# The up-projections of two squared-ReLU layers as seven block products in place of eight

## The chip, the cores and the metric

The kernel runs on one NeuronCore of one Trainium2 chip. The core has five engines that take their own instructions in order and meet only through semaphores: TensorE (PE in the profile; PEld is its weight load), VectorE (DVE), ScalarE (ACT), GpSimd (POOL) and SyncE (SP), which here only issues DMAs. Matrix products read SBUF and write PSUM; DVE and ACT read PSUM and SBUF. The metric is device time in microseconds, the median of the runs.

## The reference

The program is a small encoder trunk over 512 tokens of width 1024: an attention layer and a recurrent (RG-LRU) layer, and after each a dense squared-ReLU MLP with 4096 hidden features. Only the MLP changes:

```
def rmsnorm(x, g):
    y = xf * lax.rsqrt(jnp.mean(xf * xf, axis=-1, keepdims=True) + RMS_EPS)
    return (y * g).astype(x.dtype)

def sq_relu_mlp(h, w1, w2):
    z = jax.nn.relu(jnp.einsum('bsd,df->bsf', h, w1))     # 1024 -> 4096
    return jnp.einsum('bsf,fd->bsd', z * z, w2)           # 4096 -> 1024

for layer in range(2):
    h = h + mixer(layer, rmsnorm(h, norm_mix[layer]))
    h = h + sq_relu_mlp(rmsnorm(h, norm_mlp[layer]), w1[layer], w2[layer])
return rmsnorm(h, norm_final)
```

All inputs are float32.

## The kernel before

**Layout.** The residual stream lies transposed in SBUF: eight tiles `hT[k]` of 128 features by 512 tokens. Every float32 matrix product is done as three products of a shorter float format (`mm3`, L148 to L151): an operand X is split into a high part (a cast, `XH`) and the remainder (`XL`), and a tile of the result is WH·XH + WH·XL + WL·XH, accumulated in PSUM. A matmul instruction multiplies a 128x128 piece of weights (loaded by its own LDWEIGHTS) with 128x512 values, and the result has 512 columns, one per token. So each pass over k of one 128-feature output costs 3 matmuls.

**Norms.** `Norm.feed` is called for each finished `hT[m]`: `split` makes `hnH[m]`, `hnL[m]` (ACT L168, DVE L169) without the factor 1/rms, and `square` adds up the squares. The factor is a vector over tokens; `sums` and `rstd` compute it on PE, ACT and DVE while the next product already runs, and it is applied when a result leaves PSUM.

**Weights.** All weight reads of the program stand in one list, `plan`. `fetch` takes the next unit of 128x1024 values (512 KB): a DMA on SP's queue into one of 3 raw buffers `wr` (L97), the cast to `wh` on ACT (L99), the remainder `wl` on DVE (L100); `wh` and `wl` have 5 buffers each. `want(n)` hands out the next n units and keeps 4 more ahead. The pools of `wr`, `wh` and `wl` are open during the whole program, so the units of a layer's MLP can be fetched while the layer before still runs.

**The MLP** (`mlp`, L485). Four groups of 1024 hidden features. `up(g, u)` computes 256 features of the group: two PSUM tiles, each 8 values of k times 3 matmuls of 512 columns; `relu2` takes each through DVE (L495, max and factor), ACT (L497, square), DVE (L500, cast `zH`) and DVE (L501, remainder `zL`). `down(g, u)` multiplies the group's eight z tiles with w2 and adds the result to two tiles of `hT` (L527). After the first group, `up` of the next group and `down` of this one alternate. In the last layer the last group's `down` runs in two halves of 256 tokens each (matmuls of 256 columns, L556), so that the final norm of the first half can run beside the second.

**Order.** The code is recorded by a tile framework which then places the instructions of each engine by its own estimate of when they can run; at run time each engine takes them strictly in the order placed. Tiles come from pools; a pool that is closed gives its SBUF space to the next one opened, and the first write into that space waits for the last use of the old tiles there. Between the attention layer and MLP 0 stands a short block of 22 tiny vector operations (L457 to L471, pool `sp`), the softplus that the recurrent layer needs later.

PSUM has eight banks, four with the tag `mm` (function `mmp`) and four with the tag `at` (`atp`); attention uses both, the MLP only `mm` and two short-lived `at` tiles for the norm.

Of the kernel before, what the change touches and what calls it, by code (L numbers as in the profile page):

```python
# [40 lines left out]
def trunk(ctx: ExitStack, tc: tile.TileContext, xT, cols, win, wqkv, wo, rwin, rga, rgx, rwo, w1, w2, out):  # L41
# [37 lines left out]

    plan = []  # L80
    state = {"next": 0, "ready": []}
    AHEAD = 4

    def fetch():
        i = state["next"]
        state["next"] += 1
        nk, srcs = plan[i]
        n = nk * sum(src.shape[1] for src in srcs)
        pool = state["extra"] if i >= len(plan) - 3 else wsp
        raw = wraw.tile([P, 1024], F32, name=f"wr{i}", tag="wr")  # L90
        H = pool.tile([P, 1024], F32R, name=f"wh{i}", tag="wh")
        L = pool.tile([P, 1024], F32R, name=f"wl{i}", tag="wl")
        rv = raw[:, :n].rearrange("p (k c) -> p k c", k=nk)
        c0 = 0
        for src in srcs:
            w = src.shape[1]
            nc.sync.dma_start(rv[:, :, c0 : c0 + w], src.rearrange("(k p) c -> p k c", p=P))  # L97
            c0 += w
        S.copy(H[:, :n], raw[:, :n])  # L99
        V.tensor_sub(L[:, :n], raw[:, :n], f(H[:, :n]))  # L100
        state["ready"].append((nk, H[:, :n].rearrange("p (k c) -> p k c", k=nk), L[:, :n].rearrange("p (k c) -> p k c", k=nk)))

    def want(n):
        while len(state["ready"]) < n + AHEAD and state["next"] < len(plan):
            fetch()
# [4 lines left out]
    def add(src, r0, c0, nk):  # L110
        for h in range(0, nk, 4):
            plan.append((4, [src[r0 + h * P : r0 + (h + 4) * P, c0 : c0 + U]]))

    def add_qk(p):
        for part in range(2):
            plan.append((KT, [wqkv[:, part * D + p * P : part * D + (p + 1) * P]]))
# [4 lines left out]
    def add_wo(r):  # L121
        for u in range(2):
            plan.append((2, [wo[r * P : (r + 2) * P, u * T : (u + 1) * T]]))

    for k0, nk in FIRST:
        plan.append((nk, [wqkv[k0 * P : (k0 + nk) * P, part * D : part * D + U] for part in range(2)]))
# [4 lines left out]

    def add_mlp(layer):
        a = [(w1[layer], 0, g * D + u * U, KT) for g in range(4) for u in range(4)]
        b = [(w2[layer], g * D, u * U, KT) for g in range(4) for u in range(4)]
        seq = a[:4]
        for i in range(12):
            seq += [a[4 + i], b[i]]
        for s_ in seq + b[12:]:
            add(*s_)
# [6 lines left out]
    add_mlp(1)  # L146

# [12 lines left out]


    class Norm:
        def __init__(self, name, gain, c0=0, n=T):
            self.name, self.gain, self.acc, self.last, self.c, self.n = name, gain, None, None, slice(c0, c0 + n), n

        def split(self, k):
            g = cst[:, self.gain + k : self.gain + k + 1]
            S.activation(hnH[k], hT[k], AF.Copy, scale=g)  # L168
            V.scalar_tensor_tensor(hnL[k], hT[k], g, f(hnH[k]), ALU.mult, ALU.subtract)  # L169
# [21 lines left out]
        def sums(self):  # L191
            nt = self.n // P
            ss = atp(f"{self.name}ss")
# [10 lines left out]
        def rstd(self):  # L204
            nt = self.n // P
            row = atp(f"{self.name}row")
# [10 lines left out]
    nm1 = Norm("nm1", C_MLP0)  # L217
# [266 lines left out]

    def mlp(ly, norm, nxt, halves):  # L485
        with ExitStack() as mctx:
            zp = mctx.enter_context(tc.tile_pool(name=f"z{ly}", bufs=2))
            if halves:
                state["extra"] = mctx.enter_context(tc.tile_pool(name="wx", bufs=3))
                fin = mctx.enter_context(tc.tile_pool(name="fin", bufs=4))  # L490
            z, r, held = {}, [], []

            def relu2(g, fi, acc):
                t1 = zp.tile([P, T], F32, name=f"t1{ly}{g}{fi}", tag="t1")
                V.scalar_tensor_tensor(t1, acc, 0.0, r[0], ALU.max, ALU.mult)  # L495
                t2 = zp.tile([P, T], F32, name=f"t2{ly}{g}{fi}", tag="t2")
                S.activation(t2, t1, AF.Square)  # L497
                zH = zp.tile([P, T], F32R, name=f"zH{ly}{g}{fi}", tag=f"zH{fi}")
                zL = zp.tile([P, T], F32R, name=f"zL{ly}{g}{fi}", tag=f"zL{fi}")
                V.tensor_copy(zH, t2)  # L500
                V.tensor_sub(zL, t2, f(zH))  # L501
                z[g, fi] = (zH, zL)

            def up(g, u):
                WH, WL = want(2)
                xs = [(hnH[k], hnL[k]) for k in range(KT)]
                accs = [mmp(f"u{ly}{g}{2 * u + i}") for i in range(2)]
                if g == 0 and u == 0:
                    project(accs, PAIR, WH, WL, xs)
                    norm.sums()  # L510
                    held.extend(accs)
                    return
                for i in range(2):
                    project(accs[i : i + 1], PAIR[i : i + 1], WH, WL, xs)
                    if held:
                        r.append(norm.rstd())
                        for fi in range(2):
                            relu2(0, fi, held.pop(0))
                    relu2(g, 2 * u + i, accs[i])

            def down(g, u):
                WH, WL = want(2)
                for i in range(2):
                    m = 2 * u + i
                    acc = mmp(f"d{ly}{g}{m}")
# [218 lines left out]
```

## Time and profile before

| | us |
|---|---|
| median of 3 runs (1113.29 to 1114.4) | 1113.7 |
| the profiled execution | 1114.19 |
| its span, first to last instruction | 1112.1 |
| PE busy | 1095.4 (99%) |
| DVE busy | 665.5 (60%) |
| ACT busy | 443.0 (40%) |
| first and last start of an up-projection matmul, both layers (tile u) | 249.9 to 1043.5 |
| first and last start of a down-projection matmul (tile d) | 306.3 to 1101.6 |
| recurrent layer's products (tiles xb to ro) | 600.0 to 747.6 |

The mean granted TensorE clock of the execution was 0.997 of full speed. A group in the profile is one line, engine, operation and tile name, with count, busy time and mean duration of one; matmuls overlap in the pipeline, so the mean duration of one matmul (389 ns) is longer than the distance from one start to the next, and it is this distance that counts. "Idle before" is what the engine waited, and for whom.

### The profile page before, as it was taken

The page shows a single profiled execution, that of the slowest core. Times are in us where ns is not written, and L with a number is a line of the kernel's source. Part 1 is how long each engine was busy: PE and PEld are TensorE (multiplying, and loading weights), DVE is VectorE, ACT ScalarE, POOL GpSimd, SP SyncE. Part 2 cuts the span into 40 slices and gives each one's busy share as a digit, 9 for nine tenths or more (in the row PEclk, how much of TensorE's full clock was granted, in tenths as well). Part 3 has the DMA queues.
Part 4 walks back from the last instruction along what each step waited for, and adds up shares of the span by engine and source line. Part 5 has one row for each costly group of instructions (what it writes and reads, how often), then busy time and mean ns, then how long its engine had stood idle before and what let it go on. Part 6 is the DMA issues. An engine that isn't in the chain of part 4 may idle for free.

```text
span 1112.1 us, 13697 instructions
## 1 busy us (share of the span) xinstructions
PE 1095.4 (99%) x5368; PEld 926.3 (83%) x5368; DVE 665.5 (60%) x1108; ACT 443.0 (40%) x698; POOL 9.4 (1%) x28
## 2 busy tenths in 40 slices
PE   9999999999999999999999999899999999999997
PEld 7889988878888888888888888788888888888896
DVE  6898887878544444445455889864544454444434
ACT  6766656555322221222234687542312222222311
POOL 1010000000000000000000000000000000000000
PEclk9999999999999999999999999999999999999998
DMA  8433332222332323223233221433233332323302
GB/s 266 134 101 90 107 102 80 92 66 87 94 114 77 114 86 104 95 95 103 87 114 114 76 76 57 132 94 96 87 103 95 95 99 91 114 77 114 105 10 76
DMA packets 112752, 108.95 MB, mean 98 GB/s; under 512 B 4016, under 2 KB 108592, under 8 KB 112688
## 3 DMA queue, kind: packets, MB, share of 16 engines
q1 hardware_dynamic: 112544, 108.02, 31.8%
q8 instruction: 42, 0.69, 0.3%
q14 instruction: 22, 0.18, 0.1%
q10 hardware_dynamic: 144, 0.07, 0.0%
HBM read 101.78 MB, written 2.10 MB: 93 GB/s over the span
## 4 chain that ended last, share of the span: by engine, by line
PE 90%; DVE 6%; ACT 2%; issue 1%; DMA 1%; SPq 0%; DVEq 0%; ACTq 0%
PE d L151 11%; PE d L149 11%; PE d L150 11%; PE u L149 10%; PE u L151 10%; PE u L150 10%; PE x L344 2%; PE xb L149 1%; PE xb L151 1%; PE xb L150 1%; PE wo L149 1%; PE ro L149 1%; PE ro L150 1%; PE ro L151 1%; PE v L149 1%
## 5 line engine op out<-in xcount | busy, mean ns | idle before, releaser
L99 ACT CAST wh<-wr 128x1024 fp32r<-128x1024 f32 (+1 forms) x185 | 193.4, 1048 | 335.8 <-PE d L150 198.0
L100 DVE TENSOR_TENSOR wl<-wr,wh 128x1024 fp32r<-128x1024 f32 (+1 forms) x185 | 225.2, 1218 | 132.6 <-ACT wh L99 131.8
L150 PE MATMUL d<-zL,wh 128*128 128x512 f32 (+1 forms) x576 | 210.6, 366 | 0.0
L149 PE MATMUL d<-zH,wh 128*128 128x512 f32 (+1 forms) x576 | 210.6, 366 | 0.0
L151 PE MATMUL d<-zH,wl 128*128 128x512 f32 (+1 forms) x576 | 210.5, 365 | 0.0
L149 PE MATMUL u<-hnH,wh 128*128 128x512 f32 x512 | 199.7, 390 | 1.4 <-DVE hT L295 1.4
L151 PE MATMUL u<-hnH,wl 128*128 128x512 f32 x512 | 199.2, 389 | 0.0
L150 PE MATMUL u<-hnL,wh 128*128 128x512 f32 x512 | 199.2, 389 | 0.0
L150 PEld LDWEIGHTS d<-zL,wh 128*128 128x128 f32 x576 | 108.7, 189 | 17.6
L151 PEld LDWEIGHTS d<-zH,wl 128*128 128x128 f32 x576 | 108.7, 189 | 17.4
L149 PEld LDWEIGHTS d<-zH,wh 128*128 128x128 f32 x576 | 108.7, 189 | 17.4
L149 PEld LDWEIGHTS u<-hnH,wh 128*128 128x128 f32 x512 | 96.1, 188 | 21.5 <-ACT wh L99 1.8
L151 PEld LDWEIGHTS u<-hnH,wl 128*128 128x128 f32 x512 | 96.1, 188 | 20.1
L150 PEld LDWEIGHTS u<-hnL,wh 128*128 128x128 f32 x512 | 96.1, 188 | 19.9
L497 ACT ACTIVATE t<-t 128x512 f32<-128x512 f32 x64 | 40.4, 633 | 148.5 <-DVE t L495 148.2
L527 DVE TENSOR_TENSOR hT<-d,hT 128x512 f32<-128x512 f32 x56 | 38.7, 692 | 81.2 <-PE d L151 81.2
L495 DVE SCALAR_TENSOR_TENSOR t<-u,nm2r 128x512 f32<-128x512 f32 x32 | 22.0, 691 | 57.2 <-PE u L151 51.4
L495 DVE SCALAR_TENSOR_TENSOR t<-u,nm1r 128x512 f32<-128x512 f32 x32 | 22.0, 691 | 55.7 <-PE u L151 51.4
L501 DVE TENSOR_TENSOR zL<-t,zH 128x512 fp32r<-128x512 f32 x64 | 44.3, 692 | 2.0
L324 ACT ACTIVATE p<-p,mx 128x128 f32<-128x128 f32 (+1 forms) x64 | 35.2, 552 | 15.1 <-DVE mx L321 15.0
L500 DVE CAST zH<-t 128x512 fp32r<-128x512 f32 x64 | 27.1, 423 | 21.4 <-ACT t L497 21.2
L149 PE MATMUL v<-wh,hnH 128*128 128x256 f32 x128 | 36.7, 287 | 0.0
(292 smaller groups left out, 1568.4 us busy)
## 6 DMA issues: line engine op xcount, KB each, us to landing
wr<-in_w SPq DMA_DIRECT2D x128, 512.0 KB, 3.7
wr<-in_wqkv SPq DMA_DIRECT2D x20, 512.0 KB, 3.9
wr<-in_rwin SPq DMA_DIRECT2D x16, 512.0 KB, 3.5
wr<-in_wo SPq DMA_DIRECT2D x8, 512.0 KB, 3.5
wr<-in_rwo SPq DMA_DIRECT2D x8, 512.0 KB, 3.4
hT<-in_xT SPq DMA_DIRECT2D x8, 256.0 KB, 4.7
bias<-in_win SPq DMA_DIRECT2D x4, 512.0 KB, 4.2
kh<-kh SPq DMA_DIRECT2D x16, 128.0 KB, 2.3
```

The costliest lines, as they stand in the source:

```text
L99: S.copy(H[:, :n], raw[:, :n])
L100: V.tensor_sub(L[:, :n], raw[:, :n], f(H[:, :n]))
L149: PE.matmul(acc, WH, XH, start=start, stop=False)
L150: PE.matmul(acc, WH, XL, start=False, stop=False)
L151: PE.matmul(acc, WL, XH, start=False, stop=stop)
L324: S.activation(pt[:, seg[t] : seg[t] + n], pt[:, seg[t] : seg[t] + n], AF.Exp, bias=mx[:, t : t + 1], accum_out=sm[:, t : t + 1],)
L344: PE.transpose(b[:, c : c + P], pt[:, seg[t] + kt * P : seg[t] + (kt + 1) * P], ident)
L495: V.scalar_tensor_tensor(t1, acc, 0.0, r[0], ALU.max, ALU.mult)
L497: S.activation(t2, t1, AF.Square)
L500: V.tensor_copy(zH, t2)
L501: V.tensor_sub(zL, t2, f(zH))
L527: V.tensor_add(hT[m], acc, hT[m])
```

## The change

**Blocks.** The 4096 hidden features are worked in eight groups of 512 (before: four of 1024). For a group, the weight block (1024 inputs x 512 features) is cut into four quarters of 512 x 256, and the tokens and inputs of the normed stream into four quarters of 512 inputs x 256 tokens. In place of eight products of quarters, seven products are made (one level of Strassen's scheme), of sums of weight quarters with sums of stream quarters; the four quarters of the result are sums of the seven.

**Weight sums.** `plan` now names a kind per unit. For a group, the unit "11" issues four DMAs into four raw tiles `b11`, `b21`, `b22`, `b12` (pool `sr`, one buffer each, open only during the MLP). The kinds "s1", "s2", "s4" add raw tiles in place on DVE (L115, L116: four additions of 128x1024 in all), and each of the seven kinds is then cast and split like any unit (ACT L118, DVE L119). So a group has 7 units of w1 in place of 4; w2 has 4 units per 512 features as before. `wh` and `wl` get 4 further buffers (pool `wx`), 7 units are kept ahead in place of 4, and a `stop` mark keeps `fetch` from taking an MLP's units before that MLP begins: `prefetch(6)` stands at its start, after the pools are opened.

**Stream sums.** `Norm.split` of the tiles k < 4 works in halves of 256 tokens and stores first half and difference of the halves (L208 to L211); `sums_of`, four times at the start of each MLP, makes three further sums and their splits (L541 to L556).

**Products.** `product` (one of seven) makes two result tiles of 128 features x 256 tokens, each 4 values of k times 3 matmuls of 256 columns: 24 matmuls. `up(g)` runs the seven and adds their results up on DVE (7 operations of 512 columns) and ACT (one copy, `w`); `relu2` runs twice per group on 1024 columns, the cast `zH` now on ACT. The seven products use the `at` banks. `down(g, m)` sums over 4 z tiles in place of 8, so it runs twice as often, and so does the addition to `hT`. The order of a group on PE is p1, p5, two downs of the group before, p2, down, p4, down, p6, down, p3, down, p7, two downs.

```diff
     def fetch():
...
+        kind, nk, srcs = plan[i]
+        pool = wsp
+        if state["more"] is not None:
+            pool = state["more"] if state["units"] % 9 >= 5 else wsp
+            state["units"] += 1
...
+            if kind == "11":
+                for name, src in zip(("11", "21", "22", "12"), srcs):
+                    raws[name] = state["raw"].tile([P, 1024], F32, name=f"b{name}_{i}", tag=f"b{name}")
+                    nc.sync.dma_start(raws[name].rearrange("p (k c) -> p k c", k=4), src.rearrange("(k p) c -> p k c", p=P))
+
+            for name, at_, with_ in (("s1", "21", "22"), ("s2", "22", "11"), ("s4", "12", "22")):
+                if kind == name:
+                    if kind == "s1":
+                        V.tensor_add(raws["11"], raws["11"], raws["21"])
+                    V.tensor_add(raws[at_], raws[at_], raws[with_])
+            raw = raws[{"s1": "21", "s2": "22", "s3": "11", "s4": "12"}.get(kind, kind)]
         S.copy(H[:, :n], raw[:, :n])
         V.tensor_sub(L[:, :n], raw[:, :n], f(H[:, :n]))
...
+    def prefetch(n):
+        while len(state["ready"]) < n and state["next"] < len(plan) and state["next"] != state["stop"]:
+            fetch()
+
     def want(n):
-        while len(state["ready"]) < n + AHEAD and state["next"] < len(plan):
-            fetch()
+        prefetch(n + state["ahead"])
...
     def mlp(ly, norm, nxt, halves):
         with ExitStack() as mctx:
...
+            sr, wx, zp, tp, cp = pool("sr", 1), pool("wx", 4), pool("z", 2), pool("t", 1), pool("c", 1)
+            state.update(raw=sr, more=wx, units=0, ahead=7, stop=starts[ly + 1] if ly + 1 < len(starts) else None)
+            prefetch(6)
...
+            def sums_of(k):
...
+                V.scalar_tensor_tensor(raw[:, 2], hT[k + 4][:, HI], g2, a[:, HI], ALU.mult, ALU.subtract)
+                V.tensor_add(raw[:, 1], raw[:, 2], a[:, LO])
+                V.scalar_tensor_tensor(raw[:, 0], hT[k + 4][:, LO], g2, raw[:, 1], ALU.mult, ALU.subtract)
+                S.activation(H[:, 0:2], raw[:, 0:2], AF.Copy, scale=-1.0)
+                V.scalar_tensor_tensor(L[:, 0:2], raw[:, 0:2], -1.0, f(H[:, 0:2]), ALU.mult, ALU.subtract)
+                S.copy(H[:, 2], raw[:, 2])
+                V.tensor_sub(L[:, 2], raw[:, 2], f(H[:, 2]))
...
+            def product(acc, xs):
+                WH, WL = want(1)
+                for j in range(2):
+                    for k, (XH, XL) in enumerate(xs):
+                        mm3(acc[:, j * U : (j + 1) * U], WH(k, PAIR[j]), WL(k, PAIR[j]), XH, XL, k == 0, k == 3)
...
+                one("1", B11)
+                S.copy(w, acc["1"])
+                yield
+                one("5", t1)
+                yield
+                one("2", B21)
+                V.tensor_add(cA[:, :, LO], acc["2"], w)
+                yield
+                one("4", t4)
+                yield
+                one("6", t2)
+                V.tensor_add(w, acc["6"], w)
+                V.tensor_add(cA[:, :, HI], acc["5"], w)
+                yield
+                one("3", B22)
+                V.tensor_add(cA[:, :, HI], acc["3"], cA[:, :, HI])
+                relu2(g, 0, cA, ALU.max, r[0])
+                yield
+                one("7", t3)
+                V.tensor_add(w, acc["7"], w)
+                V.tensor_add(cB[:, :, LO], acc["4"], w)
+                V.tensor_add(cB[:, :, HI], acc["5"], w)
+                relu2(g, 1, cB, ALU.min, r[0])
```

**How the change moves instructions.** First place: SP's queue at the end of the attention layer (kh, kl are the last copies of attention; wr is a raw buffer; the number after a name tells one buffer's contents from another's). Before:

```order
L253 DMA kl70_2235<-kl70_2235 64x512 [waits DVE_49]
L253 DMA kl71_2241<-kl71_2241 64x512 [waits DMAHW2_49,DVE_49]
L97 DMA wr33_2546<-in_w1 128x4x256 [waits DMAHW4_49,DVE_49]
L97 DMA wr34_2605<-in_w1 128x4x256 [waits DMAHW5_49,DVE_49]
L97 DMA wr35_2672<-in_w1 128x4x256 [waits DMAHW6_49,DVE_49]
```

Now:

```order
L295 DMA kl71_2241<-kl71_2241 64x512 [waits DMAHW2_49,DVE_49]
L104 DMA wr42_3007<-in_w2 128x4x256 [waits DMAHW4_49,DVE_49]
L104 DMA wr44_3075<-in_w2 128x4x256 [waits DMAHW5_49,DVE_49]
L104 DMA wr47_3186<-in_w2 128x4x256 [waits DMAHW6_49,DVE_49]
L110 DMA b11_33_2839<-in_w1 128x4x256 [waits DMAHW1_49,DMAHW2_49,DMAHW0_49,DMAHW7_49,DVE_49,Activation_49]
L110 DMA b21_33_2841<-in_w1 128x4x256
L110 DMA b22_33_2843<-in_w1 128x4x256
L110 DMA b12_33_2845<-in_w1 128x4x256
```

Before, the first reads of MLP 0's w1 wait for raw buffers that the units of the attention layer's last projection set free. Now the first read of w1 is `b11_33`, and its wait on DVE counts, in the built program, up to L512, the operation of the softplus block that reads that block's pool last: the tiles of `sr` lie where the pools of attention and the pool `sp` lay.

Second place: VectorE at the start of MLP 0, now (tL are splits of the stream sums, sp4 and sp8 the end of the softplus block, wl33 the remainder for p1, wl34 for p5, wl35 for p2, wl36 for p4, wl37 for p6):

```order
L554 SCALAR_TENSOR_TENSOR tL03_2912<-ht03_2913,tH03_2911 128x512 [waits Activation_49]
L510 TENSOR_TENSOR sp4_103<-sp4_103,sp2_2787 128x8 [waits DVE_49]
L512 SCALAR_TENSOR_TENSOR sp4_103<-sp4_103,sp1_2786 128x8 [waits DVE_49]
L513 TENSOR_SCALAR sp8_104<-sp4_103 128x8 [waits DVE_49]
L119 TENSOR_TENSOR wl33_2838<-b11_33_2839,wh33_2837 128x1024 [waits DMAHW6_49,Activation_49]
L115 TENSOR_TENSOR b11_33_2839<-b11_33_2839,b21_33_2841 128x1024 [waits DMAHW7_49,DVE_49]
L116 TENSOR_TENSOR b21_33_2841<-b21_33_2841,b22_33_2843 128x1024 [waits DMAHW0_49,DVE_49]
L119 TENSOR_TENSOR wl34_2850<-b21_33_2841,wh34_2849 128x1024 [waits Activation_49]
L119 TENSOR_TENSOR wl35_2856<-b12_33_2845,wh35_2855 128x1024 [waits DMAHW1_49,Activation_49]
L119 TENSOR_TENSOR wl36_2860<-b22_33_2843,wh36_2859 128x1024 [waits Activation_49]
L116 TENSOR_TENSOR b22_33_2843<-b22_33_2843,b11_33_2839 128x1024 [waits DVE_49]
```

All four `sums_of` and the whole softplus block stand ahead of the first weight remainder; before, five units of w1 (wl33 to wl37, L100) stood ahead of the softplus block's second operation. On ACT likewise the cast `wh33` stands behind the last cast of the stream sums. In MLP 1 the same `b11` (unit 145) waits for the last matmul of `ro7`, the recurrent layer's output product, and ACT's `wh145` and DVE's `wl145` stand among the first two stream sums.

Third place: VectorE late in a middle group, now (group 4 of MLP 0; p7 is the seventh product, d036 and d037 the last two downs of group 3, zL041 the second remainder of z of group 4, which the first down of group 4 reads):

```order
L618 TENSOR_TENSOR w04_4304<-p704_4605,w04_4304 128x512 [waits PE_49]
L119 TENSOR_TENSOR wl90_4644<-b22_84_4437,wh90_4643 128x1024 [waits Activation_49]
L619 TENSOR_TENSOR cB04_4303<-p404_4457,w04_4304 128x2x256 [waits DVE_49]
L620 TENSOR_TENSOR cB04_4303<-p504_4337,w04_4304 128x2x256
L632 TENSOR_TENSOR hT6_80<-d036_4648,hT6_80 128x512 [waits PE_49]
L578 SCALAR_TENSOR_TENSOR cB04_4303<-cB04_4303,nm1r_3041 128x1024 [waits DVE_49]
L119 TENSOR_TENSOR wl91_4681<-wr91_4682,wh91_4680 128x1024 [waits DMAHW5_49,Activation_49]
L632 TENSOR_TENSOR hT7_81<-d037_4662,hT7_81 128x512 [waits PE_49]
L116 TENSOR_TENSOR b12_84_4439<-b12_84_4439,b22_84_4437 128x1024
L583 TENSOR_TENSOR zL041_4640<-cB04_4303,zH041_4639 128x1024 [waits Activation_49]
```

Between the end of p7 and `zL041` DVE now takes nine operations: four of the group's own sums and `relu2`, two additions to `hT`, two weight remainders and one weight addition. Before, a z tile's remainder followed its product after one operation on PSUM and a cast.

195 lines of the change are left out of this document (114 added, 81 removed).

## The prediction

> **What bounds the kernel now.** I read the page first, then who made TensorE wait, then the middle of the MLP.
>
> ```profile
> span 1112.1 us, 13697 instructions
> PE 1095.4 (99%) x5368; PEld 926.3 (83%) x5368; DVE 665.5 (60%) x1108; ACT 443.0 (40%) x698; POOL 9.4 (1%) x28
> PE 90%; DVE 6%; ACT 2%; issue 1%; DMA 1%; SPq 0%; DVEq 0%; ACTq 0%
> ```
>
> The chain of waits that ended last is 90% TensorE. The waits of TensorE alone, longest first:
>
> ```profile
> PE ro L149 <- ACT gdH L649: 1.6, 1, 1.6
> PE ro L149 <- DVE y L644: 1.5, 1, 1.5
> PE u L149 <- DVE hT L295: 1.4, 1, 1.4
> ```
>
> In both MLPs there is one wait that counts, 1.4 us at the start of the first. Between 300 and 600 us (windows: span, then busy us of PE, PEld, DVE, ACT, POOL, clock, DMA share, GB/s) TensorE is never idle, while VectorE works 139.83 of 300 us:
>
> ```profile
> 300.00:600.00 300.00, 300.00 (x1325) 248.51 (x1324) 139.83 (x171) 80.70 (x94) 0.00 (x0) 1.00 0.31 96
> ```
>
> So matmul columns are the time, as long as the other engines keep up. The change gives TensorE fewer columns and VectorE more work; the questions are what a column costs in shorter matmuls, and where VectorE's cover ends.
>
> **Matmuls removed.** The distance from start to start counts, not the duration. From the timeline, 20 starts of 512 columns and 53 of 256 columns:
>
> ```profile
> 499.62 0.39 PE L150 MATMUL u<-hnL,wh 128*128 128x512 f32 x1
> ...
> 503.92 0.39 PE L151 MATMUL d<-zH,wl 128*128 128x512 f32 x1
> ```
>
> ```profile
> 1069.72 0.28 PE L149 MATMUL d<-zH,wh 128*128 128x256 f32 x1
> ...
> 1075.96 0.28 PE L150 MATMUL d<-zL,wh 128*128 128x256 f32 x1
> ```
>
> 4.30/19 = 226.3 ns and 6.24/52 = 120.0 ns, each matmul with its own weight load. Per 512 features the up-projection had 4 x 8 x 3 = 96 matmuls of 512 columns, 21.7 us; now 7 x 24 = 168 of 256 columns, 20.2 us (one product 2.88). That is 1.56 us per group, 25.0 us for 16 groups, where an eighth of the columns would be 2.7 per group: a matmul of 256 columns takes 6.9 ns more than half of one of 512. `down` keeps its columns (one `down` of 12 matmuls: 2.72 us), but in the last layer only the last 512 features run in halves: 96 matmuls of 512 and 192 of 256 (21.7 + 23.0) for 384 of 256 (46.1), 1.3 us less. **Together -26.3 us.**
>
> [...]
>
> **VectorE and ScalarE in a middle group.** Rows by form, and stretches of VectorE's timeline, where operations behind each other start closer than their duration:
>
> ```profile
> L100 DVE TENSOR_TENSOR wl<-wr,wh 128x1024 fp32r<-128x1024 f32 x183 | 223.8, 1224 | 132.3 <-ACT wh L99 131.5
> L99 ACT CAST wh<-wr 128x1024 fp32r<-128x1024 f32 x183 | 192.2, 1052 | 335.7 <-PE d L150 198.0 <-PE u L150 90.9 <-PE wo L150 11.5
> L500 DVE CAST zH<-t 128x512 fp32r<-128x512 f32 x64 | 27.1, 423 | 21.4 <-ACT t L497 21.2
> ```
>
> ```profile
> 240.92 1.89 DVE L295 TENSOR_TENSOR hT<-wo,hT 128x512 f32<-128x512 f32 x3 [0.84 <-PE wo L151]
> ...
> 253.39 0.74 DVE L169 SCALAR_TENSOR_TENSOR hnL<-hT,cst,hnH 128x512 fp32r<-128x512 f32 x1
> 254.06 0.68 DVE L182 TENSOR_TENSOR nm1acc<-nm1acc,nm1sq 128x512 f32<-128x512 f32 x1
> 254.66 0.68 DVE L295 TENSOR_TENSOR hT<-wo,hT 128x512 f32<-128x512 f32 x1
> ...
> 255.33 1.22 DVE L100 TENSOR_TENSOR wl<-wr,wh 128x1024 fp32r<-128x1024 f32 x1
> 256.47 0.16 DVE L458 TENSOR_TENSOR sp<-cst,sp 128x8 f32<-128x8 f32 x1
> ...
> 259.16 0.17 DVE L460 TENSOR_SCALAR sp<-sp 128x8 f32<-128x8 f32 x1
> ...
> 264.51 0.17 DVE L471 TENSOR_SCALAR sp<-sp 128x8 f32<-128x8 f32 x1
> ...
> 1105.53 3.22 DVE L553 SCALAR_TENSOR_TENSOR nf1o<-hT,cst,nf1row 128x256 f32<-128x256 f32 x8 [1.32 <-PE nf1row L208]
> ```
>
> Steps: 1.14 us for 1024 columns, 0.60 for a sum of 512, 0.66 for a scaled one of 512, 0.40 for a scaled one of 256, some 0.35 for a plain one of 256. A group now has on VectorE 11 remainders, 4 weight sums, 2 `relu2` and 2 zL of 1024 columns (19 x 1.14 = 21.7) and 7 sums of products and 8 additions to hT (15 x 0.60 = 9.0): 30.7 us, against 20.2 + 21.7 = 41.9 us of TensorE. ScalarE has 15 operations of 1.05 and a copy, 16.4 us. So in the middle neither is the bound. The tightest chain is z: behind p7 VectorE's nine operations and zL take 8.7 us (4 x 1.14 and 5 x 0.60 as in the third place shown, and zL 1.14); TensorE has until then two downs, p1, p5 and half a down, 5.4 + 5.8 + 1.4 = 12.6 us. Casts stand some 20 us ahead of their product. I take **0** here; without the cover of 3.9 us each us would cost 14 us over the run.
>
> **Start of MLP 0.** Here the change moves work into a place where nothing covers it. TensorE's last wo matmul and first u matmul now:
>
> ```profile
> 248.08 0.39 PE L151 MATMUL wo<-oH,wl 128*128 128x512 f32 x1
> ...
> 249.90 0.47 PE L149 MATMUL u<-hnH,wh 128*128 128x512 f32 x1 [1.44 <-DVE hT L295]
> ```
>
> In the changed order the first w1 read waits for the end of the softplus block, and that stands on VectorE behind all norm rows and all stream sums. From the first hT addition (240.9): 15 sums of 512 (9.0), 4 differences of 256 (1.4), 8 scaled of 256 (3.2) and 4 scaled of 512 (2.6) end the norm at 257.1. Stream sums: four times 0.40 + 0.35 + 0.40 + 0.66 + 0.35 = 8.6. The 20 softplus rows from 259.16 to 264.51 took 5.5 us less one wl, 4.4; between other work they cost between 0.08 and 0.2 each, I take 2.8. With 0.8 for waits on ACT (one table load), the read is issued at **269.3**. Then:
>
> ```profile
> wr<-in_w SPq DMA_DIRECT2D x128, 512.0 KB, 3.7
> 10.00:15.00 5.00, 5.00 (x22) 3.85 (x21) 5.00 (x8) 5.00 (x9) 0.00 (x0) 1.00 1.04 363
> ```
>
> About 4 us for `b11` (four reads of 2.1 MB at 363 GB/s: 5.8 us), 1.05 for the cast: p1 can begin at 274.5, its third matmul waits for wl33 until 275.8; p5 waits for two weight sums, a cast and a remainder, until 280.6. From there VectorE leads: until zL of group 0 it has 26 operations of 1024 columns for 11 units and sums of two groups and w2 units (18 wl, 8 sums), 8 of 512, and 4 for relu2 and zL: 30 x 1.14 + 8 x 0.60 = 39 us, starting 5.3 after the read, and some 5 of waits on casts and on group 1's reads, whose buffers come free only now: until 49.7 us after the read. TensorE's work in that time is 11 products, 30 matmuls of 512 and the norm's 0.9: 39.4. Lost: 269.3 - 248.3 = 21.0, and 10.3; less the 1.6 lost now: **+29.7 us**. Bounds: softplus rows hidden and no waits, 22; durations in place of steps, 39.
>
> The clock is no further cost:
>
> ```profile
> 1103.00:1106.00 3.00, 1.84 (x10) 1.49 (x10) 0.64 (x3) 0.26 (x1) 0.00 (x0) 0.74 0.00 0
> 1106.00:1112.00 6.00, 0.00 (x0) 0.00 (x0) 2.75 (x8) 0.00 (x0) 0.00 (x0) 0.50 0.52 175
> ```
>
> An idle TensorE falls to 0.50, so p1 may take 5.8 us; it then ends when p5's remainder is ready.
>
> **Start of MLP 1.** `b11` waits only for the last ro matmul. From there VectorE has the last hT, hnL and sum (2.0), the stream sums (8.6), the same 30 operations of 1024 (34.2) and 8 of 512 (4.8): 49.6, some 2 of waits, against TensorE's 39.4: **+12 us** (bounds 8, if TensorE's rows fall better between; 20, by durations). Now nothing is lost there.
>
> **Ends.** Behind group 7 each down takes 2.72 us, and VectorE has 1.86 per tile for hT, hnL and the squares, beside zL and some remainders: nearly full. 0 to 4, taken as **+2**.
>
> **Sum.** -26.3 + 29.7 + 12 + 2 = +17.4 on the profiled execution's 1114.2 (span 1112.1; 0.5 above the median of 1113.7): 1131.6; on the median's scale **1131 us**.
>
> **Rivals.** (a) VectorE binds in the middle too: zL later than 12.6 us behind p7. For it: VectorE at 73% of the time, in strict order, with waits on casts between. Against: 3.9 us of slack. At 2 us in each of 14 groups: 1159. (b) Faster: the starts cost less than the 26.3 gained. The mechanism would be that VectorE takes sums that touch only SBUF at the rate of the CAST row (423 ns for 512 columns): stream sums and weight sums fall by 40%, 7 us at each start, which with the low bounds (22 and 8) leaves 16: 1114.2 - 26.3 + 16 = 1104. The nm1acc row, SBUF only, 0.68 us for 512, speaks against it. It decides once both starts together cost under 26.3 us. (c) The shorter matmuls don't pay: above 226.3 x 96/168 = 129 ns the seven products are a loss. At 188 ns (the mean of a weight load, were it not hidden) +158 us, 1315. Against: 120.0 measured, weights changing each time. [...]
>
> **Numbers.** Forecast 0.80, with its bounds as the range: 1114.2 - 26.3 + 22 + 8 + 0 = 1118, and 1114.2 - 26.3 + 39 + 20 + 4 = 1151, on the median's scale 1117 to 1151. (a) 0.10; (b) 0.07; (c) 0.01; 0.02 that the starts cost just what the matmuls gain and the time stays within 0.2% (2.2 us, about what a measurement of this kernel can tell from no change). The forecast's low edge adds 0.01 to that. Faster 0.07, same 0.03, slower 0.90. The range leaves out (b), (c) and the larger part of (a), under 2 in 10.
>
> **What would show it.** PE's waits: `p1..` of MLP 0 on DMA, ACT or DVE for over 20 us, a gap of some 26 us behind wo; at MLP 1 some 6 us and pieces on wl. In the middle windows PE full and DVE near 75%. Starts of the products' matmuls 120 ns apart. DVE busy for some 900 us in all: 665, and 48 more remainders and 64 weight sums (112 x 1.22 = 137), 112 sums of products and 64 additions to hT of 512 columns (some 120), less a third of the old relu2 and zH. I would be wrong if the first w1 read came long before 265 us, or if TensorE waited for zL or wl in every group.

## The result, and the profile after

The changed kernel takes **1130.96 us** (median of 4 runs, 1128.77 to 1133.38); the kernel before, in the same runs, 1113.61 us (1113.29 to 1114.4). The ratio is **1.0155, 95% interval 1.0133 to 1.0178**: slower. Predicted were 1131 us, range 1117 to 1151. The profiled execution took 1131.64 us, with a mean granted clock of 0.982 (0.997 before).

The page of the changed kernel: the span, the busy time of each engine, the shares of the chain that ended last.

```profile
span 1129.8 us, 16086 instructions
PE 1080.1 (96%) x6424; PEld 962.4 (85%) x6424; DVE 880.6 (78%) x1324; ACT 537.7 (48%) x794; POOL 10.5 (1%) x28
PE 84%; DVE 10%; ACT 2%; DMA 2%; issue 2%; DVEq 0%; ACTq 0%; SPq 0%
```

TensorE is busy for 15.3 us less than before (1095.4), and the span is 17.7 us longer: what the shorter matmuls saved was more than lost again in idle time. TensorE's share of the chain fell from 90% to 84%, VectorE's rose from 6% to 10%. Whom TensorE waited for (us in total, times, longest):

```profile
PE p L180 <- ACT wh L118: 32.5, 4, 24.7
PE p L182 <- DVE wl L119: 3.4, 5, 1.3
```

In the MLPs the kernel before had one wait of 1.4 us, at the start of MLP 0, and no other ahead of the final norm. Now one wait of 24.7 us stands there. The timeline around it, row by row from four engines: VectorE's softplus row for which the read waits (L512), SP's queue with the first w1 read, ScalarE's cast, VectorE's remainder and TensorE's p1:

```profile
267.53 0.17 DVE L512 SCALAR_TENSOR_TENSOR sp<-sp,sp 128x8 f32<-128x8 f32 x1
...
267.76 2.02 SPq L110 DMA_DIRECT2D b<-in_w  x4
...
271.85 1.04 ACT L118 CAST wh<-b 128x1024 fp32r<-128x1024 f32 x1 [5.25 <-DMA b<-in_w]
...
272.93 1.23 DVE L119 TENSOR_TENSOR wl<-b,wh 128x1024 fp32r<-128x1024 f32 x1 [5.02 <-ACT wh L118]
...
272.95 0.58 PE L180 MATMUL p<-hnH,wh 128*128 128x256 f32 x1 [24.70 <-ACT wh L118]
```

The read is issued 0.2 us behind the start of that softplus row, as the order had said, and 4.1 us later the cast starts. Windows of the changed kernel (span, then busy us of PE, PEld, DVE, ACT, POOL; clock, DMA share, GB/s): the gap, the middle of each MLP, and two short stretches that come back below, one in MLP 0 and one at the start of MLP 1:

```profile
249.00:275.00 26.00, 1.59 (x5) 1.30 (x6) 20.67 (x60) 13.56 (x23) 0.00 (x0) 0.57 0.24 78
340.00:590.00 250.00, 250.00 (x1573) 226.98 (x1572) 187.13 (x201) 96.08 (x98) 0.00 (x0) 1.00 0.32 98
830.00:1080.00 250.00, 250.00 (x1573) 226.96 (x1572) 190.36 (x204) 96.13 (x97) 0.00 (x0) 1.00 0.31 95
304.00:307.00 3.00, 3.00 (x16) 3.00 (x15) 3.00 (x4) 2.94 (x4) 0.00 (x0) 0.50 0.09 20
772.00:778.00 6.00, 5.48 (x26) 5.20 (x25) 6.00 (x9) 3.87 (x7) 0.00 (x0) 0.50 0.36 115
```

In the middle TensorE is full, VectorE at 75%. A group has 7 x 24 + 8 x 12 = 264 matmuls, and from the first matmul of p1 in one group to that in the next it is 42.04 us (428.06 and 470.10; predicted 41.9). By stages, the loss is therefore at the openings. Two stages suffice for all runs: MLP 0 from the last wo matmul's start to the first xb matmul's, and from there to the end of the span (the recurrent layer, 147.8 us from its first to its last matmul's start in both kernels, and MLP 1).

| kernel | median us | MLP 0 | first xb to the end |
|---|---|---|---|
| before | 1113.6 | 351.9 | 512.1 |
| changed | 1131.0 | 370.5 | 511.5 |
| e1 softplus tiles apart | 1119.7 | 357.9 | 512.6 |
| e2 and five units early | 1099.4 | 350.2 | 500.2 |
| e3 no weight sums | 1122.1 | 366.4 | 507.7 |
| e4 two raw buffers | 1127.6 | 368.5 | 510.7 |
| e5, e6, e10: 2, 6, 12 more on z | 1129.0, 1139.5, 1159.0 | 368.8, 372.5, 386.4 | 511.8, 518.5, 524.0 |
| e7 e2 and extra matmuls | 1102.6 | 350.5 | 502.7 |
| e8 e2 and squares on GpSimd | 1106.5 | 351.7 | 505.5 |
| e9 e2, first group plain | 1098.3 | 348.9 | 501.2 |
| e11 e9, stream sums apart | **1093.7** | 342.8 | 502.6 |
| e12 e11, in both MLPs | 1094.8 | 343.0 | 502.1 |

The stages are of one profiled execution each; what lies ahead of them ended between 246.5 and 248.3 us, so a difference below 1 us says nothing. In e11's 502.6 matmuls of the recurrent layer's ro took up to 628 ns, in the other executions at most 505, and its first row of matmuls ran 46.6 us from first to last start (693.2 to 739.8), in e12 44.9. Of eight groups the matmuls save 12.5 us per MLP, so the opening of MLP 0 cost 370.5 - 351.9 + 12.5 = **31.1 us**, and in MLP 1, with its 1.3 us more at the end, opening and end cost 511.5 - 512.1 + 13.8 = **13.2 us**.

### The profile page after: what moved, and what is told of

Read it like the earlier page. It is cut to its first block, busy times and chain, and to the rows that moved or that the text cites. A ratio compares the mean times of both kernels' runs of the same rounds, so it can differ in the third digit from the quotient of the medians.

```text
span 1129.8 us, 16086 instructions
## 1 busy us (share of the span) xinstructions
PE 1080.1 (96%) x6424; PEld 962.4 (85%) x6424; DVE 880.6 (78%) x1324; ACT 537.7 (48%) x794; POOL 10.5 (1%) x28
## 4 chain that ended last, share of the span: by engine, by line
PE 84%; DVE 10%; ACT 2%; DMA 2%; issue 2%; DVEq 0%; ACTq 0%; SPq 0%
PE d L180 10%; PE d L181 10%; PE d L182 10%; PE p L182 8%; PE p L180 8%; PE p L181 8%; DVE wl L119 2%; DMA b<-in_w 2%; PE x L386 1%; PE xb L180 1%; PE xb L182 1%; PE xb L181 1%; PE wo L180 1%; PE wo L182 1%; PE wo L181 1%
## 5 line engine op out<-in xcount | busy, mean ns | idle before, releaser
L118 ACT CAST wh<-b 128x1024 fp32r<-128x1024 f32 x112 | 115.6, 1048 | 223.6 <-DVE b L116 92.0
L180 PE MATMUL p<-hnH,wh 128*128 128x256 f32 x512 | 147.8, 289 | 32.6 <-ACT wh L118 32.5
L119 DVE TENSOR_TENSOR wl<-b,wh 128x1024 fp32r<-128x1024 f32 x112 | 135.1, 1221 | 44.7 <-ACT wh L118 44.6
L118 ACT CAST wh<-wr 128x1024 fp32r<-128x1024 f32 (+1 forms) x121 | 125.5, 1040 | 90.3 <-PE p L181 46.1
L119 DVE TENSOR_TENSOR wl<-wr,wh 128x1024 fp32r<-128x1024 f32 (+1 forms) x121 | 146.5, 1211 | 19.4 <-ACT wh L118 18.9
L182 PE MATMUL p<-hnH,wl 128*128 128x256 f32 x512 | 147.4, 289 | 3.4 <-DVE wl L119 3.4
L181 PE MATMUL p<-hnL,wh 128*128 128x256 f32 x512 | 147.3, 288 | 0.0
L180 PEld LDWEIGHTS p<-hnH,wh 128*128 128x128 f32 x512 | 100.6, 196 | 35.6 <-ACT wh L118 34.1
L180 PE MATMUL p<-tH,wh 128*128 128x256 f32 x384 | 108.8, 283 | 0.0
L182 PE MATMUL p<-tH,wl 128*128 128x256 f32 x384 | 108.7, 283 | 0.0
L181 PE MATMUL p<-tL,wh 128*128 128x256 f32 x384 | 108.6, 283 | 0.0
L181 PEld LDWEIGHTS p<-hnL,wh 128*128 128x128 f32 x512 | 100.7, 197 | 1.5
```

Of the source, the lines that this page charges most:

```text
L180: PE.matmul(acc, WH, XH, start=start, stop=False)
L181: PE.matmul(acc, WH, XL, start=False, stop=False)
L182: PE.matmul(acc, WL, XH, start=False, stop=stop)
```

## The experiments

**What makes the opening of MLP 0.** The prediction's theory: the first w1 read waits for SBUF that the softplus tiles hold, and those rows stand behind all of VectorE's other work. The rival: VectorE's rows themselves set the start, and the wait only stands in front of them.

```diff
-    with tc.tile_pool(name="sp", bufs=1) as sp:
-        e, ng, zz, z2 = (sp.tile([P, KT], F32, name=f"sp{i}") for i in range(4))
+    if True:
+        e, ng, zz, z2 = (per.tile([P, KT], F32, name=f"sp{i}") for i in range(4))
```

> The softplus tiles get memory of their own, so the first w1 read of MLP 0 (b11_33) waits only for the last wo matmul (247.9 us) and no longer for the last softplus row (267.5). Nothing else is taken away: VectorE has the same rows. Theory (the wait for the shared memory is the larger part of the loss at MLP 0): the read lands at about 252, p1 begins at about 253.5 as soon as cast and hnH are there, and only what VectorE cannot do in time is left, as at the start of MLP 1 (12 us predicted). MLP 0 becomes about 18 us shorter, the whole 1112 to 1116. Rival (VectorE's own rows, stream sums and weight sums, set the start and the wait only stands in front of them): less than 6 us is gained, 1125 or more, and PE's gap splits into waits for wl and the stream sums.

1119.73 us (1118.5 to 1122.42), 1.0062 of before, interval 1.0047 to 1.0077: 11.2 us less than the changed kernel, some two thirds of what the theory had said, and between the ranges of the two. The timeline of this kernel's TensorE and VectorE shows where the larger part of the rest stayed:

```profile
250.02 1.89 DVE L337 TENSOR_TENSOR hT<-wo,hT 128x512 f32<-128x512 f32 x3
...
252.94 0.58 PE L180 MATMUL p<-hnH,wh 128*128 128x256 f32 x1 [5.68 <-ACT wh L118]
...
256.74 0.69 DVE L224 TENSOR_TENSOR nm1acc<-nm1acc,nm1sq 128x512 f32<-128x512 f32 x1
257.34 1.22 DVE L119 TENSOR_TENSOR wl<-b,wh 128x1024 fp32r<-128x1024 f32 x1
...
258.61 0.58 PE L182 MATMUL p<-hnH,wl 128*128 128x256 f32 x1 [4.88 <-DVE wl L119]
```

p1's first matmul starts 20 us earlier than in the changed kernel, but its third needs the remainder `wl`, and that stands on VectorE behind the last additions to hT and the norm rows, at 257.34. MLP 0 became 12.6 us shorter and its opening still costs 18.5, not the 12 of MLP 1: ahead of MLP 0 VectorE is late by itself, which the late read had covered. Both were right in part.

**The reads and units brought forward.** The first group's blocks go through the buffers `wr`, which are open all the time, so five units can be prepared while the layer before still runs.

```diff
+                state["first"] = i in starts
...
+                    if i in starts:
+                        raws[name] = wraw.tile([P, 1024], F32, name=f"b{name}_{i}", tag="wr")
...
-    state["stop"] = starts[0]
+    state["stop"] = starts[0] + 5
```

> As the run before, and the first group's w1 blocks of both layers are read into the buffers of the plain units, so that their read needs no memory that comes free at the end of the stage before: five units (b11, its first sum, b12, b22 and the second sum) are prepared while wo or ro still runs. Theory (read, first cast and first remainders are the rest of the opening's cost): p1, p5 and p2 follow the last wo matmul as soon as hnH and hnL are there, TensorE waits then for the stream sums only, 8 to 12 us lost at MLP 0 and 3 to 6 at MLP 1: 1098 to 1107, below the kernel before. Rival (VectorE's work at the opening is the same whenever it is done, and what is prepared early is only missing later): no gain beyond the run before, 1111 to 1116.

**1099.43 us** (1099.02 to 1100.05), 0.9877 of before, interval 0.9862 to 0.9891. Its waits between 245 and 345 us:

```profile
PE p L187 <- ACT tH L560: 2.5, 1, 2.5
PE p L187 <- ACT hnH L210: 1.5, 1, 1.5
PE p L188 <- DVE hnL L211: 1.1, 2, 0.7
PE p L187 <- DVE hT L344: 0.6, 1, 0.6
```

No wait is left for wh or wl, 3.2 us for the late hT and norm rows, 2.5 for the stream sums. The part from the first xb on became 11.3 us shorter: at MLP 1 the read that waited for the last ro matmul, and what came late behind it, was nearly all of the 13.2 us. The run brings two things forward at once, the read and the casts and remainders of five units, and does not tell their shares apart. The opening of MLP 0 costs 10.8 us now. So the same products, with their first weights ready, beat the kernel before.

**VectorE's share of it.** The four weight sums of a group are left out.

```diff
-                    if kind == "s1":
-                        V.tensor_add(raws["11"], raws["11"], raws["21"])
-                    V.tensor_add(raws[at_], raws[at_], raws[with_])
+                    pass
```

> All four weight sums of every group are left out (the products then use the plain blocks, so the output is not the reference's): 64 rows of 1.22 us less on VectorE, 4.6 of its 30.7 us of a middle group. Theory (in the middle TensorE alone is the time, with 75% of VectorE used): the middle windows stay at 42.0 us per group, and only the openings gain, 8 sums each of which some 3 to 9 us count: 1115 to 1126. Rival (VectorE sets the pace of the middle too, through z): 4.6 us for each of 14 groups, about 1067 to 1075.

1122.09 us (1121.46 to 1122.9): 8.9 us less than the changed kernel, 4.1 in MLP 0 and 3.8 in MLP 1 by the profile. The middle window of this kernel, the same as the changed kernel's above:

```profile
340.00:590.00 250.00, 250.00 (x1573) 226.97 (x1572) 164.33 (x178) 94.12 (x97) 0.00 (x0) 1.00 0.31 98
```

VectorE has 22.8 us less work in 250 than in the changed kernel, and TensorE does the same 1573 matmuls; a group takes 42.04 us here too. In the middle VectorE's work costs nothing, at an opening 8 weight sums (9.8 us) cost some 4. At MLP 0 these 4 are not the sums' length as such: the waits of group 1 in the next paragraph, and the half clock at 304 us behind them, are gone in this kernel.

**The single raw buffer.** In the changed kernel p1 of group 1 waited 0.7 us for its remainder and p5, the product behind it, 2.2 us at 301 us for a weight sum (the expectation below takes that wait for p1's). Their reads could be issued only when group 0 had let go of the raw tiles:

```profile
287.23 1.50 SPq L110 DMA_DIRECT2D b<-in_w  x2
...
303.20 0.39 PE L180 MATMUL p<-hnH,wh 128*128 128x256 f32 x1 [2.18 <-ACT wh L118]
```

```diff
-            sr, wx, ... = pool("sr", 1), pool("wx", 4), ...
+            sr, wx, ... = pool("sr", 2), pool("wx", 2), ...
```

> The w1 blocks get two raw buffers each instead of one, paid for by two prepared units fewer (7 in place of 9). Group 1's b11 read then need not wait for group 0's sum and remainder. Theory (the 2.2 us wait of p1 of group 1 at 300 us, and part of the idle time of VectorE there, come from the single raw buffer): 2 to 4 us less at MLP 0, at most 2 at MLP 1, if two units fewer cost nothing in the middle: 1126 to 1130. Rival (VectorE's order, not the read, is late there): within 1 us of the changed kernel's 1131, or above it by what the missing units cost.

1127.55 us (1126.75 to 1127.91), 3.4 less than the changed kernel. Between 245 and 345 us the 24.5 us and 0.5 us for wl are the only waits left; MLP 0 is 2.0 us shorter, of the rest 0.9 lies ahead of MLP 0 and says nothing. The two prepared units fewer are missed in the middle: two short waits for wh (0.4 and 0.3 us) stand in each MLP, and four groups take 169.6 us (381.74 to 551.37) in place of 168.2. So the opening itself gained about 3.5 us.

**The slack in the middle.** The prediction gave the z chain 3.9 us of slack. Two, six and twelve idle operations (cB times 1.0) are put behind p7:

```diff
                 V.tensor_add(cB[:, :, HI], acc["5"], w)
+                if g >= 2:
+                    for _ in range(6):
+                        V.tensor_scalar(cB, cB, 1.0, None, ALU.mult)
```

> Two more VectorE operations of 1024 columns (cB times 1.0) stand between the last sum behind p7 and relu2 in every group from the third on, some 2.3 us longer for the z chain, 35 rows of 42 us busy per group in place of 31. Theory (z has 3.9 us of slack behind the 8.7 us chain, and TensorE alone is the time in the middle): the middle windows stay full, the time within 1 us of the changed kernel's 1131, apart from the end, where the last down waits up to 2 us longer. Rival (VectorE paces the middle): 2.3 us for each of 6 groups of two layers, about 1158.

> Six such operations in place of two, some 6.8 us on the z chain and 37.6 of 42 us busy. Theory: the slack of 3.9 us is used up and some 3 us are lost in each of 12 groups, with waits of PE's down on zL: 1160 to 1180. Rival (the slack is larger than worked out, since the scheduler's order lets other products stand in front of the down): no loss in the middle, below 1140.

> As e6_more6 with twelve extra VectorE operations of 1024 columns per group on the z chain; each took 0.60 us there (SBUF alone, one input), so six were only 3.6 us, still inside the predicted slack of 3.9, and the middle stayed full. Twelve are 7.2 us. Theory (slack 3.9): 3.3 us are lost in each of the 12 groups and some 7 more at the two ends than with six, 1139 + 40 + 7, about 1175 to 1190, with waits of d on z in the middle windows. Rival (more slack than worked out, or other products fill the wait): the middle stays full, below 1155.

One execution each: 1128.95, 1139.49 and 1158.97 us. An extra operation took 0.69 us and a step of 0.60, half of what was put into the first two expectations, so the three are 1.2, 3.6 and 7.2 us. With two the time lies among the changed kernel's own runs; with six the end of each MLP is longer (2.0 us in the first stage, 7.0 in the second), the middle is not: a group takes 42.03 us. Its middle window:

```profile
345.00:595.00 250.00, 250.00 (x1560) 226.38 (x1560) 204.82 (x233) 93.39 (x95) 0.00 (x0) 1.00 0.34 103
```

With twelve, the middle of both MLPs, then the extra rows as a group, then its wait for z over the whole span:

```profile
345.00:595.00 250.00, 245.58 (x1527) 221.59 (x1526) 214.86 (x252) 90.78 (x94) 0.00 (x0) 0.99 0.32 98
845.00:1095.00 250.00, 247.74 (x1549) 223.65 (x1548) 220.42 (x258) 93.12 (x95) 0.00 (x0) 1.00 0.31 95
```

```profile
L623 DVE TENSOR_SCALAR cB<-cB 128x1024 f32<-128x1024 f32 x144 | 99.1, 688 | 1.8
```

```profile
PE d L180 <- ACT zH L582: 20.7, 6, 7.0
```

Six stay inside the slack, as the prediction has it. With twelve the time lies between the ranges of theory and rival: 3.3 us over the slack, some 20 us should be lost per window; 4.4 and 2.3 are. The placed order shows why: in the program with twelve, the first four downs of a group are cut in two, six matmuls each on the z half that is ready, and the other six come only behind p6, where the program as changed has twelve in a row. The framework knew of the longer chain and moved other products in front of it. Two thirds of the waits for z, 14 of 20.7 us, stand where no product is left to move, one of 7.0 us behind group 7 of each MLP. So the middle had more slack than the sum gave it, and the ends have little.

**The clock.** In the early kernel TensorE runs at half clock from 258.9 to 272.6 us. Twelve extra matmuls were meant to fill its wait there.

```diff
+                    if g == 0 and n == "4":
+                        for _ in range(12):
+                            PE.matmul(acc[n][:, :U], hnH[7][:, :P], hnL[7][:, LO], start=True, stop=True)
                     product(acc[n], xs)
```

> The early kernel (e2_early), with 12 extra matmuls of 256 columns on hnH and hnL of the last tile ahead of p4 of group 0, into its own bank, which p4's first matmul then overwrites; they stand where TensorE waits 2.5 us for the stream sums at half clock. Theory (the clock does cost at the opening, against the prediction's step): the half clock ends some 4 us after 259 in place of 272.3, some 25 matmuls go 0.09 us faster: 1096 to 1098 in place of 1099.4. Rival (VectorE sets the opening, the clock is free as predicted): 1099 to 1101.

1102.59 us (1102.2 to 1102.86), 3.2 more than the early kernel and outside both ranges. The run does not tell the two apart: the framework placed the extra matmuls not into the wait (263.6 to 266.2) but behind it, after a matmul of the norm:

```profile
273.66 1.05 PE L257 MATMUL nm1row<-ident,rt 128*128 128x128 f32 x8
274.47 1.68 PE L602 MATMUL p<-hnL,hnH 128*128 128x256 f32 x12
```

There they cost their own 1.5 us in each MLP. By the stages MLP 0 is 0.3 us longer and the rest 2.5: in MLP 0 this execution left half clock at 269.4 in place of 272.6, before the extra matmuls ran (10.2 us of half clock; the some 4 us of the theory were an estimate), and at the opening of MLP 1 TensorE waited 0.9 us more. What the clock costs can be read from the early kernel's own trace: behind its last wait, from 266.6 to 272.6, 27 matmuls ran at half clock, some 2.4 us longer in all, and no later wait up to 345 us could have covered it.

**Work moved to GpSimd.** GpSimd is idle at the opening, so the seven additions of squares per norm go there.

```diff
-                V.tensor_add(self.acc, self.acc, sq)
+                (G if self.name in ("nm1", "nm2") else V).tensor_add(self.acc, self.acc, sq)
```

> The early kernel (e2_early), with the seven additions of the sums of squares of the norms ahead of both MLPs on GpSimd in place of VectorE. Theory (VectorE's rows set what is left of the opening of MLP 0, 10.8 us): 7 x 0.60 = 4.2 us less on VectorE between 245 and 259, of which 2 to 4 come off the end: 1095 to 1098. Rival (the two engines get in each other's way, or the sum ends so late on GpSimd that rstd and z wait for it): 1099 or more, with longer VectorE rows beside GpSimd's.

1106.52 us (1105.7 to 1107.05), 7.1 more than the early kernel: the rival. Of this kernel the group on GpSimd, two pairs of VectorE's rows from the timeline, and one of TensorE's waits:

```profile
L231 POOL TENSOR_TENSOR nm1acc<-nm1acc,nm1sq 128x512 f32<-128x512 f32 x7 | 11.9, 1704 | 76.5 <-ACT nm1sq L230 76.3
```

```profile
245.86 1.44 DVE L215 TENSOR_TENSOR nm1d<-hT 128x256 f32<-128x256 f32 x1
...
249.54 0.41 DVE L215 TENSOR_TENSOR nm1d<-hT 128x256 f32<-128x256 f32 x1
...
257.38 2.29 DVE L123 TENSOR_TENSOR b<-b,b 128x1024 f32<-128x1024 f32 x1
...
261.26 1.21 DVE L123 TENSOR_TENSOR b<-b,b 128x1024 f32<-128x1024 f32 x1
```

```profile
PE nm1ss L246 <- POOL nm1acc L231: 2.7, 1, 2.7
```

An addition took 1.70 us there in place of 0.69, and several of VectorE's rows beside it grew by about a microsecond each: the same difference of 256 columns takes 0.41 and 1.44 us, the same weight sum 1.21 and 2.29. Beside the row of 0.41 us there is a GpSimd addition too (248.44 to 251.10), and there the addition was the one that grew, to 2.66 us; the shortest took 1.27. The rows show operations of both engines growing beside each other; what makes them grow they do not show. On top of it TensorE waited 2.7 us for the last sum, which now ends later. By the stages, though, only 1.5 of the 7.1 us lie in MLP 0 and 5.3 behind the first xb: at the opening of MLP 1 TensorE waited 2.9 us for the stream sums and a copy, in place of 0.9. These waits do not account for all of the 5.3.

**Less for VectorE at the opening of MLP 0.** The first group of the first layer is computed as eight plain products (192 matmuls of 256 columns in place of 168), so that no sum is needed before group 1.

```diff
+                if g == 0 and layer in PLAIN0:
+                    up_ = [("plain", 4, [w1[layer][rows[k], cs[c]]]) for c in range(2) for k in range(2)]
...
+            for n, _ in enumerate(eight() if plain0 else up(0)):
...
+                if plain0 and n < 4:
+                    sums_of(n)
```

> The early kernel (e2_early), with the first group of the first MLP alone as eight plain block products (no stream sums, no weight sums, 4 prepared units in place of 7, C12 = A11 B11 - A11 (B11 - B12) + A12 B22); the stream sums are made behind it, for group 1. TensorE gets 24 matmuls of 256 columns more, 2.9 us; VectorE has 4 weight sums, 3 remainders and the 8.6 us of stream sums, some 16 us, less in front of the first product that needs them. Theory (VectorE's rows in the opening of MLP 0 are what is left of its cost, 10.8 us): TensorE no longer waits for stream sums, only for the last hT rows (1 to 3 us), and stays at full clock: 10.8 falls to 4 to 6 with the extra product in it, 1093 to 1096 in place of 1099.4. Rival (the work put off is missed in group 1, whose sums and units then come late): no gain, 1099 to 1103, with waits of p in group 1.

1098.29 us (1097.8 to 1099.86), 0.9860 of before, interval 0.9844 to 0.9877: only 1.1 us below the early kernel, just below the rival's range. Its longest waits between 245 and 350 us:

```profile
PE p L190 <- ACT cB L649: 2.5, 1, 2.5
PE d L190 <- ACT zH L595: 1.5, 1, 1.5
PE p0b L190 <- DVE hT L347: 0.6, 1, 0.6
```

The waits for stream sums are gone and those for norm rows down to 0.2 us; two new ones stand in group 1, on the buffer `cB` that the stream sums now held until 288 us, and on the z that came late from it. Two causes could give that: the buffer, or too much work for VectorE in that stretch.

```diff
-                raw = cp.tile([P, 2, T], F32, name=f"ht{ly}{k}", tag="cB" if k % 2 or plain0 else "cA")
+                raw = cp.tile([P, 2, T], F32, name=f"ht{ly}{k}", tag="hs" if plain0 else ..., bufs=2 if plain0 else 1)
```

> As e9_plain_first, where TensorE's gap moved to group 1 (2.5 us on cB, whose memory the stream sums held until 287, and 1.5 us on the z that came late from it): the stream sums of the first MLP get two buffers of their own, paid for by one prepared unit fewer (8 in place of 9). Theory (the shared buffer, not VectorE's amount of work, was what group 1 waited for): 3 to 4.5 us less, 1093.5 to 1095.5. Rival (VectorE's amount of work between 255 and 300 is the limit, and the wait only changes its name): within 1 us of e9_plain_first's 1098.3.

> As e11_own_sums, with the first group of the second MLP as eight plain products too. There TensorE waited only 0.9 us in all at the opening of the early kernel (e2_early), so the extra product's 2.9 us buy nothing: 2 to 3 us slower than e11_own_sums. Rival (the opening of MLP 1 still loses time that no wait shows): the same or faster.

**1093.67 us** (1093.08 to 1095.04), **0.9821 of before, interval 0.9808 to 0.9835**: it was the buffer. In this kernel TensorE has one wait between 245 and 350 us, and the stretch that had been the gap reads:

```profile
PE p0b L190 <- DVE hT L347: 0.6, 1, 0.6
```

```profile
260.00:265.00 5.00, 5.00 (x44) 5.00 (x44) 5.00 (x10) 2.72 (x6) 0.00 (x0) 1.00 0.00 0
265.00:270.00 5.00, 5.00 (x44) 5.00 (x44) 4.95 (x6) 4.53 (x7) 0.00 (x0) 1.00 0.49 153
270.00:275.00 5.00, 5.00 (x44) 5.00 (x43) 5.00 (x12) 2.62 (x5) 0.00 (x0) 1.00 0.49 165
```

TensorE and VectorE are both full, at full clock. The opening of MLP 0 costs 342.8 - 351.9 + 12.5 = 3.4 us, 2.9 of them the eighth product. The same in both MLPs took 1094.79 us (1094.47 to 1095.2; 0.9833, interval 0.9820 to 0.9847), 1.1 more where 2 to 3 were expected; the intervals overlap, and whether the extra product costs anything in MLP 1 is not settled.

## Why the prediction was right, point by point

- **Matmuls, -26.3.** Right. Starts of the products' matmuls lie 0.12 us apart (303.42, 303.54, 303.66 in the changed kernel), a middle group takes 42.04 us for 41.9.
- **Middle, 0.** Right: full windows, VectorE at 75%, and a kernel with 22.8 us less for VectorE per window goes no faster in them (e3). Too small was the slack behind it: "each us would cost 14 us" beyond 3.9 did not come, because the framework places other products in front of a late z.
- **Opening of MLP 0, +29.7.** 31.1 measured. The read was worked out for 269.3 and issued at 267.8; the cast, at 273.3 by the prediction, started at 271.9. The second half of z of group 0, where the sum ends, was ready 51.0 us after the read (zL ends at 318.7), for 49.7 (the parts as written, 5.3, 39 and 5, make 49.3). But TensorE never waited for z there. What it lost behind the read was 5.2 us until p1, 3.3 in later waits for weights (0.5, 0.7 and 2.2) and 2.7 at half clock (1.2 of them for p1, in place of a wait; next point), 11.2 in place of the 10.3 predicted; that the two came so close is in part luck. And the division was not right: "269.3 - 248.3 = 21.0" for the late read suggests that 21 us go with it. Taken away, it gave 12.6 (e1), since VectorE's norm rows alone hold the first remainder until 257.3. The rest came away in two further steps, 7.7 with units prepared early (e2) and 7.4 net of the eighth product (e9 and e11). The waits of 0.7 and 2.2 us come from the single raw buffer (e4), which the prediction had among its "some 5 of waits".
- **"The clock is no further cost".** Wrong in part. For p1 it held: TensorE ran at half clock until 276.7, some 1.2 us more, and p5 began at 279.1, when its remainder had just ended (279.0), so that a faster p1 would only have waited. But the 2.2 us wait at 301 was followed by a second stretch at 0.50, the fourth of the windows of the changed kernel: from 304.0 to 307.4 a matmul took 0.213 us in place of 0.12, 16 times, 1.5 us that no term had. And at MLP 1, behind a wait of 5.0 us, a third stretch ran from 771.6 to 778.5 (the fifth window), some 2.2 us more, of which later waits for weights (0.5, 0.6 and 1.3 us) may have covered a part.
- **Opening of MLP 1 and ends, +12 and +2.** 13.2 in all, of which 7.9 are waits for weights at the opening; no run tells the end's share. Its read waited for the last ro matmul, as said; with the first units early 11.3 of it went (e2).
- **The rivals.** (a) VectorE in the middle: excluded by e3 and by the six extra rows of e6. (b) It rested on SBUF-only sums at 423 ns for 512 columns; weight sums took 1.22 us for 1024. What was true of it is the point from which it decides: once the openings cost less than the matmuls gain the kernel is faster, and e2, e7 to e9, e11 and e12 got there by other means. (c) 0.12 us per matmul, far below 0.129.
- **VectorE's total**: 880.6 us, "some 900" predicted.

## What to carry to other kernels

A change that takes work from the busiest engine and gives it to another was decided here where the other has no cover, at the openings of its stages: cost those separately, and list every row that the other engine has from the end of the stage before. When a long wait is taken away, ask what stands behind it: here the 21 us of a late read hid some 8 us of VectorE's other work, norm rows first, and behind the work put off to mend those stood a shared buffer. The first units of a stage belong into buffers that are open while the stage before still runs, and where a stage's preparation is long, its first group may use the plain form.

## What the runs showed of the hardware that was not expected

- **Half clock after short waits, but not after each.** A wait of 2.2 us (301.0 to 303.2, changed kernel) was followed by 3.4 us at half clock, which began 0.8 us after TensorE had started again. A wait of 2.5 us at 286 to 288.6 (e9) and the one of 1.4 us of the kernel before were followed by none. The early kernel and e7 had the same waits at the same places, 0.6, 0.4, 1.5 and 0.7 us between 251 and 259 and 2.5 at 264, went to half clock at 258.9 and 259.2, and left it at 272.6 and at 269.4. By the clock recorded in the traces, the stretches at half clock behind the first matmuls that end inside the kernel lasted 23.9, 3.4 and 6.8 us in the changed kernel, 13.7 in the early kernel and 10.2 in e7: 7, 1, 2, 4 and 3 times the shortest of them, 3.41 us. In the 3.4 us ahead of the stretches at 304.0, 258.9 and 259.2 TensorE was busy for 1.2, 1.0 and 1.25 us. What sets the times at which a stretch begins and ends is not shown.
- **One input or two.** On VectorE an operation of 1024 float32 columns in SBUF took 0.69 us with one tensor input (e10's group above) and 1.22 us with two (`wl`, weight sums).
- **VectorE and GpSimd.** Beside GpSimd's additions the same VectorE row took 0.41 us once and 1.44 us once, and an addition took from 1.27 to 2.66 us (e8).
